# Seven block products instead of eight for gate and up of the first feed-forward stage, and a second product that sums four tiles in PSUM

## The chip, the cores and the metric

The kernel runs on one core of one Trainium2 chip. The metric is the device time of one execution in microseconds (us): 2367.63 us is the median of three runs of the kernel before, which lie between 2363.91 and 2369.41 us. All stages of the layer run in one launch. Engines are named as in the profile: PE is TensorE (matmuls), PEld its weight loads, DVE is VectorE, ACT is ScalarE, POOL is GpSimd, and SP is the engine whose queue issues all DMAs here.

## The reference

One inference step of one encoder layer. It computes, for 1024 prompt tokens and 64 sample tokens of width 1024,

```
h = x + 0.5 * rmsnorm(swiglu(rmsnorm(x), w_gate1, w_up1, w_down1))
m = token_mix(rmsnorm(h))          # latent attention and stick-breaking attention, 8 heads each
h = h + rmsnorm(m)
h = h + 0.5 * rmsnorm(swiglu(rmsnorm(h), w_gate2, w_up2, w_down2))
y = rmsnorm(h)
swiglu(x, wg, wu, wd) = (silu(x @ wg) * (x @ wu)) @ wd      # 1024 -> 2816 -> 1024, all float32
```

with a gain in every rmsnorm. Returned are y and the new rows of the attention's caches. The change touches the feed-forward blocks (swiglu) and nothing of the mathematics of the rest.

## The kernel before, in words

Features lie on the 128 partitions, tokens on the free axis. The 1088 tokens are two groups: G1 with 576 tokens (512 of the prompt and the sample), handled in two chunks of 288 columns, and G2 with 512 tokens in one chunk. A stream of four feed-forward stages runs through the kernel: block 1 of G1, block 1 of G2, block 2 of G1, block 2 of G2. A mixing stream (attention) is woven between the steps of the second and third of them (`weave`, L149: after each step of the first generator as many steps of the second as a debt counted in TensorE work allows). The first stage has no attention beside it.

Full precision is had from three passes: each operand is split into hi (a rounded copy, ACT) and lo (the rest, DVE, or POOL for some tiles), `split` on L115 to L125, and `mm3` (L158) issues three matmuls: hi by hi, hi by lo, lo by hi. A weight tile is loaded from HBM by SP, 128 x 512 at a time (`wr`, 4 buffers), and split into `wh` and `wl` of 128 x 1024, 4 buffers each (`weight`, L236).

`ffn` (L245) goes over the 22 tiles of 128 hidden features. For each it splits a gate tile and an up tile, and for each chunk of tokens sums eight k-tiles of mm3 into one PSUM bank for gate and one for up, then forms silu by Exp, Ln, Exp on ACT (L289 to L291), two multiplications on DVE that read PSUM (L292, L293) and a split into `hh` and `hl`. Two hidden tiles make a part. `down` (L252) is the second product: for each of 8 output tiles and each chunk it sums the two tiles of a part in PSUM (6 matmuls) and adds the bank to `y` on DVE (L265); it stands between the two hidden tiles of the next part. PSUM has 8 banks, four of them (`bank_f`) for the feed-forward stream and four for the mixing stream.

The start is in `body`: the two halves (288 tokens) of G1 are loaded and normalised (`rms_pe`, L200, and `scaled`, L221); after the first half the first step of the stage is issued (L911). `prep` (from L913) loads G2, takes its norm and forms x1, the hi and lo input of the second stage, between the steps of the first. `finish` (L838) of G1 and the mixing stream follow.

The order in which instructions stand in each engine's queue is set when the program is built: the emission order gives the priority, a planner with its own durations places an instruction where it finds it ready, and a tile's buffer is reused when all its readers are done. On the chip each queue runs in that fixed order.

Of the kernel before, what the change touches and what calls it, by code (L numbers as in the profile page):

```python
# [7 lines left out]
F32 = mybir.dt.float32  # L8
# [7 lines left out]
P = 128  # L16
D = 1024
KT = D // P
SEQ = 1024
# [15 lines left out]
# token groups: (first token, tokens, chunk of the moving axis). The tokens lie as  # L35
# the first half of the prompt, the sample, the second half of the prompt.
# [4 lines left out]
# TensorE work of the feed-forward stream for one unit of the mixing stream's, part by part  # L41
# [8 lines left out]
class Layer:  # L50
    def __init__(self, tc, ctx, a):
# [4 lines left out]
        self.turn = 0  # L56
        self.work = self.share = self.debt = 0.0
# [27 lines left out]
        # keys and values: group 1 (prompt | new), group 2, cached  # L85
# [28 lines left out]
    # x = hi + lo exactly; without x, lo holds the value and is replaced in place  # L114
# [12 lines left out]
    # TensorE work is counted, for the interleaving of the two streams  # L127
# [15 lines left out]
    # a step without TensorE work in the first stream makes room for some of the second's  # L143
# [4 lines left out]
    # the steps of the first stream, with the second one's between them: self.share of its work each  # L148
# [15 lines left out]
    # a bank of the feed-forward stream  # L164
# [3 lines left out]
    # a bank of the mixing stream  # L168
# [10 lines left out]
    # sum of squares, tile by tile  # L179
# [9 lines left out]
    # 1 / sqrt(mean over all features + eps), on every partition, from the sums of squares  # L189
# [9 lines left out]
    # the same with the sums over the tiles left to TensorE (T at most 512)  # L199
# [10 lines left out]
    # tmp() gives [P, T] tiles  # L210
# [9 lines left out]
    # hi and lo of gain * src * r  # L220
# [7 lines left out]
    # y := res + gain * y * r, for one tile of features  # L228
# [16 lines left out]
    def ffn(self, pool, tmp, n, g, xhi, xlo, y, end=None, tail=None):  # L245
# [4 lines left out]
        order = [(dt, c0, C) for dt in range(KT) for c0 in range(0, T, C)]  # L250

        def down(part, first, order, beside=iter(())):  # L252
            ws = [self.weight(pool, wd[mi]) for mi, _, _ in part]
            for dt, c0, C in order:
                ps = self.bank_f()
                for i, ((wh, wl), (_, hh, hl)) in enumerate(zip(ws, part)):
                    self.mm3(ps[:, :C], wh[:, dt * P:dt * P + P], wl[:, dt * P:dt * P + P],
                             hh[:, c0:c0 + C], hl[:, c0:c0 + C], i == 0, i == len(part) - 1)
                yield True
                next(beside, None)  # L260
                yy = y[:, dt, c0:c0 + C]
                if first:
                    nc.scalar.copy(yy, ps[:, :C])
                else:
                    nc.vector.tensor_tensor(yy, ps[:, :C], yy, op=ALU.add)  # L265

        for m in range(0, FT, 2):
            part = []
            for mi in (m, m + 1):
                if mi > m and pend:  # L270
                    yield from down(pend.pop(0), m == 2, order)
                gh, gl = self.weight(pool, wg[mi])
                uh, ul = self.weight(pool, wu[mi])
                hh = pool.tile([P, T], F32R, name="hh")
                hl = pool.tile([P, T], F32R, name="hl")
                for c0 in range(0, T, C):
                    cs = slice(c0, c0 + C)
                    pg = self.bank_f()
                    for k in range(KT):
                        ks = slice(k * P, k * P + P)  # L280
                        self.mm3(pg[:, :C], gh[:, ks], gl[:, ks], xhi[:, k, cs], xlo[:, k, cs], k == 0, k == KT - 1)
                        yield True
                    pu = self.bank_f()
                    for k in range(KT):
                        ks = slice(k * P, k * P + P)
                        self.mm3(pu[:, :C], uh[:, ks], ul[:, ks], xhi[:, k, cs], xlo[:, k, cs], k == 0, k == KT - 1)
                        yield True
                    s = tmp()[:, :C]
                    nc.scalar.activation(s, pg[:, :C], AF.Exp, scale=-1.0)  # L289
                    nc.scalar.activation(s, s, AF.Ln, bias=self.one)  # L290
                    nc.scalar.activation(s, s, AF.Exp, scale=-1.0)  # L291
                    nc.vector.tensor_tensor(s, pg[:, :C], s, op=ALU.mult)  # L292
                    nc.vector.tensor_tensor(s, pu[:, :C], s, op=ALU.mult)  # L293
                    self.split(hh[:, cs], hl[:, cs], x=s)
                part.append((mi, hh, hl))
# [4 lines left out]
        if tail:  # L300
            order = [(dt, c0, tail) for c0 in range(0, T, tail) for dt in range(KT)]
        yield from down(pend.pop(0), False, order, end)
# [18 lines left out]
        # query latent  # L321
# [13 lines left out]
        # rotary key: rows 64..95 the key, rows 96..127 its halves swapped  # L335
# [14 lines left out]
        # stick-breaking queries and keys, two heads per tile  # L350
# [31 lines left out]
        # key/value latent  # L382
# [14 lines left out]
        # stick-breaking values, tokens on the partitions  # L397
# [17 lines left out]
        # latent attention: keys and values  # L415
# [60 lines left out]
    def load_values(self, pool, pair, parts):  # L476
        """[128 keys, key tile, head, hi|lo, 64]"""
# [21 lines left out]
    def scores(self, ops, n):  # L499
        """ops: list of (lhsT, rhs tile); n keys in one or two equal halves."""  # L500
# [9 lines left out]
    def stick(self, pool, ps, nh, w, n, mask):  # L510
        """weights of stick-breaking attention from the scores; the last key is never visible."""
# [9 lines left out]
        # minus the log weight: v[j] = (z[j+1] + v[j+1]) - log_beta[j]  # L521
# [66 lines left out]
    def headnorm(self, pool, o, n, row, gi, c0, sums=None, turned=None):  # L588
        """per-head RMSNorm of two heads on the partitions; sums or turned: eps * (softmax sum)^2 of each query."""
# [88 lines left out]
    def sum_rows(self, pool, total, nb):  # L678
        """eps * sum^2 of each query, repeated over the 64 rows of its head."""
# [9 lines left out]
    def sample_pair(self, pool, kind, pair):  # L689
# [9 lines left out]
        for par in range(2):  # L699
# [6 lines left out]
            # queries of this head in its own half of the columns, zeros in the other  # L706
# [54 lines left out]
        if mla:  # L761
            # row r of lhsT holds query r % 64 of head r // 64: only its own head's rows count
# [8 lines left out]
    # output projection, post norm, the residual (left in y), and the statistics of the next norm  # L771
# [30 lines left out]
def body(tc, a, ctx):  # L802
# [35 lines left out]
    def finish(gi, y, n, bank):  # L838
        """post norm and residual of a feed-forward block; after the second the final norm"""
# [18 lines left out]
    def last(gi, y, res, pool, step):  # L858
        """the same in steps of tokens, with the residual at hand"""
# [22 lines left out]
    def work(pool, T, n=4):  # L882
        """tiles for passing use, weights, and accumulators of the mixing stream"""
# [5 lines left out]
    # first feed-forward block of group 1; the input norm of group 2 lies beside it  # L889
    T1, T2 = G1[1], G2[1]  # L890
    x1 = pair(fp, T2, "x")
    with tc.tile_pool(name="x0", bufs=1) as xp:
        x0 = pair(xp, T1, "x")
        y = ytile(T1)
        half = T1 // 2
        y0 = ytile(T1)
        zero = L.ffn(F, fact, 1, G1, *x0, y0)
        for c0 in (0, half):
# [8 lines left out]
            L.run(L.scaled(tmp, lambda k: y[:, k, cs], "pre1", r, x0[0][:, :, cs], x0[1][:, :, cs]))  # L907
            # what the first half of the tokens suffices for
# [4 lines left out]
        def prep():  # L913
# [4 lines left out]
            r = yield from L.rms(tmp, L.bank_f, (get(k) for k in range(KT)), T2, D)  # L918
            yield from L.scaled(tmp, get, "pre1", r, *x1)
# [3 lines left out]
        L.run(zero)  # L923
    rx = fp.tile([P, TM], F32, name="rx")[:, :T1]
# [88 lines left out]
def layout(inp):  # L1013
    """The arrays of the launch: the inputs in the order the chip reads them, and constants of the shapes."""
# [83 lines left out]
```

## Time and profile before

| | |
|---|---|
| runs: median (lowest to highest) | 2367.63 us (2363.91 to 2369.41) |
| the profiled execution, from its first to its last instruction (span) | 2367.6 us, the only time given for it |
| PE / PEld / DVE / ACT / POOL busy | 2283.5 / 2033.4 / 1539.0 / 1244.7 / 93.6 us |
| share of the chain that ended last | PE 69%, DVE 12%, ACT 9%, DMA 4%, issue 4% |

Busy is the time in which at least one instruction of the engine runs; matmuls overlap each other, so that a mean of 0.29 us for one does not say how often one starts. In a view by line, `out<-in` names the tiles written and read, `xN` is the number of instructions, then come the busy time in us and the mean ns of one, and behind the second bar the idle time ahead of them with what ended it. A view of stretches gives for each the busy time of every engine with its instructions, the TensorE clock granted (1.00 is full), the share of time that the DMA engines were busy, and GB/s.

### The profile page before, as it was taken

To read this page: it belongs to the slowest core of one execution; us is meant where nothing else is said; L and a number is where in the kernel's file an instruction comes from. 1 tells how busy PE (TensorE), PEld (TensorE's weight loads), DVE (VectorE), ACT (ScalarE), POOL (GpSimd) and SP (SyncE) were. 2 spreads that over 40 slices of the span, in tenths; PEclk is the share of its full clock that TensorE was granted. 3 is DMA by queue.
4 is the path that set the end of the run, shared out by engine and by line. 5 is a ranking of instruction groups with operands and counts; after the bars stand their busy time and mean duration, and the time that the engine had idled before them with its cause. 6 is when DMAs were issued, how large, how long until landed. Compare 5 with 4: busy or idle time off the path is not lost.

```text
span 2367.6 us, 37687 instructions
## 1 busy us (share of the span) xinstructions
PE 2283.5 (96%) x13869; PEld 2033.4 (86%) x13869; DVE 1539.0 (65%) x2743; ACT 1244.7 (53%) x2459; POOL 93.6 (4%) x270
## 2 busy tenths in 40 slices
PE   8999999989999999999999999999999999999997
PEld 7999999879987777788778999998888888888885
DVE  5555555764277878855873488888878588555555
ACT  6543333453367777754542477777776455433333
POOL 1000000010000000000110000000000010000001
PEclk9999999999999999999999999999999999999998
DMA  6322222445453343343444632323221424333321
GB/s 210 97 95 90 81 80 90 148 144 168 161 150 113 110 129 100 95 151 111 151 142 160 188 96 79 99 72 99 72 86 62 144 81 139 128 98 98 98 90 36
DMA packets 186615, 268.81 MB, mean 114 GB/s; under 512 B 59216, under 2 KB 68048, under 8 KB 186400
## 3 DMA queue, kind: packets, MB, share of 16 engines
q1 hardware_dynamic: 186432, 266.41, 35.8%
q8 instruction: 110, 1.80, 0.3%
q14 instruction: 73, 0.60, 0.1%
HBM read 227.61 MB, written 40.88 MB: 113 GB/s over the span
## 4 chain that ended last, share of the span: by engine, by line
PE 69%; DVE 12%; ACT 9%; DMA 4%; issue 4%; SPq 1%; POOL 1%; DVEq 0%; ACTq 0%; POOLq 0%
PE f L133 46%; PE s L133 11%; PE v L133 6%; PE t L133 3%; PE t L137 2%; DVE a L526 2%; DVE a L529 1%; ACT wh L121 1%; DVE a L520 1%; ACT a L517 1%; DVE wl L122 1%; ACT a L518 1%; ACT a L519 1%; DVE y L265 1%; DVE e L224 1%
## 5 line engine op out<-in xcount | busy, mean ns | idle before, releaser
L133 PE MATMUL f<-xh,wh 128*128 128x288 f32 (+1 forms) x2112 | 695.3, 329 | 4.4 <-ACT xh L121 2.8
L133 PE MATMUL f<-xl,wh 128*128 128x288 f32 (+1 forms) x2112 | 694.3, 329 | 2.9 <-POOL xl L122 1.8
L133 PE MATMUL f<-xh,wl 128*128 128x288 f32 (+1 forms) x2112 | 692.8, 328 | 0.0
L121 ACT CAST wh<-wr 128x512 fp32r<-128x512 f32 x638 | 374.2, 617 | 524.9 <-PE f L133 376.5
L122 DVE TENSOR_TENSOR wl<-wr,wh 128x512 fp32r<-128x512 f32 x638 | 431.2, 698 | 233.0 <-ACT wh L121 208.7
L133 PEld LDWEIGHTS f<-xl,wh 128*128 128x128 f32 x2112 | 397.7, 188 | 33.7 <-POOL xl L122 3.4
L133 PEld LDWEIGHTS f<-xh,wh 128*128 128x128 f32 x2112 | 397.6, 188 | 33.3 <-ACT xh L121 3.3
L133 PEld LDWEIGHTS f<-xh,wl 128*128 128x128 f32 x2112 | 397.5, 188 | 28.1 <-issue 0.8
L133 PE MATMUL f<-hh,wh 128*128 128x288 f32 (+2 forms) x1072 | 350.7, 328 | 6.6 <-ACT hh L121 3.2
L133 PE MATMUL f<-hl,wh 128*128 128x288 f32 (+2 forms) x1072 | 350.7, 327 | 0.0
L133 PE MATMUL f<-hh,wl 128*128 128x288 f32 (+2 forms) x1072 | 349.9, 327 | 0.2 <-DVE wl L122 0.2
L265 DVE TENSOR_TENSOR y<-f,y 128x288 f32<-128x288 f32 (+2 forms) x488 | 247.9, 523 | 85.4 <-PE f L133 83.8
L133 PEld LDWEIGHTS f<-hh,wh 128*128 128x128 f32 x1072 | 201.7, 189 | 23.4 <-ACT hh L121 4.0
L133 PEld LDWEIGHTS f<-hh,wl 128*128 128x128 f32 x1072 | 202.1, 189 | 14.3 <-issue 1.0
L133 PEld LDWEIGHTS f<-hl,wh 128*128 128x128 f32 x1072 | 202.1, 189 | 13.8 <-issue 0.8
L293 DVE TENSOR_TENSOR act<-f,act 128x288 f32<-128x288 f32 (+1 forms) x132 | 70.0, 531 | 92.6 <-PE f L133 91.8
L564 DVE TENSOR_TENSOR pl<-t,ph 128x384 fp32r<-128x384 f32 (+1 forms) x160 | 101.2, 633 | 35.6 <-ACT ph L563 31.2
L563 ACT CAST ph<-t 128x384 fp32r<-128x384 f32 (+1 forms) x160 | 86.7, 542 | 57.2 <-PE t L137 54.7
L292 DVE TENSOR_TENSOR act<-f,act 128x288 f32<-128x288 f32 (+1 forms) x132 | 69.8, 529 | 66.5 <-ACT act L291 66.4
L137 PE MATMUL t<-c_ident,a 128*128 128x128 f32 x616 | 106.0, 277 | 2.7 <-ACT a L531 0.9
L133 PE MATMUL s<-kh,qh 128*128 128x256 f32 (+3 forms) x224 | 84.4, 378 | 24.0 <-DVE a L529 16.1
L121 ACT CAST hh<-act 128x288 fp32r<-128x288 f32 (+1 forms) x132 | 64.8, 491 | 66.0 <-DVE act L293 65.9
(312 smaller groups left out, 3464.7 us busy)
## 6 DMA issues: line engine op xcount, KB each, us to landing
wr<-in_wg SPq DMA_DIRECT2D x176, 256.0 KB, 2.9
wr<-in_wu SPq DMA_DIRECT2D x176, 256.0 KB, 3.0
wr<-in_wd SPq DMA_DIRECT2D x176, 256.0 KB, 3.2
wr<-in_win SPq DMA_DIRECT2D x44, 256.0 KB, 3.3
kl<-ks SPq DMA_DIRECT2D x64, 128.0 KB, 2.8
wr<-in_wout SPq DMA_DIRECT2D x32, 256.0 KB, 2.8
h<-y SPq DMA_DIRECT2D x16, 288.0 KB, 2.3
p<-in_xT SPq DMA_DIRECT2D x16, 256.0 KB, 3.4
```

The costliest lines, as they stand in the source:

```text
L121: nc.scalar.copy(hi, x)
L122: eng.tensor_tensor(lo, x, f(hi), op=ALU.subtract)
L133: self.nc.tensor.matmul(out, lhsT=lhsT, rhs=rhs, start=start, stop=stop)
L137: self.nc.tensor.transpose(out, x, ident)
L224: self.nc.vector.scalar_tensor_tensor(x, src(k), self.gain(name, k), r, op0=ALU.mult, op1=ALU.mult)
L265: nc.vector.tensor_tensor(yy, ps[:, :C], yy, op=ALU.add)
L292: nc.vector.tensor_tensor(s, pg[:, :C], s, op=ALU.mult)
L293: nc.vector.tensor_tensor(s, pu[:, :C], s, op=ALU.mult)
L517: nc.scalar.activation(av, z, AF.Abs)
L526: nc.vector.tensor_tensor_scan(a[:, j0:n - 1][:, ::-1], zz[:, ::-1], a[:, j0:n - 1][:, ::-1], BIG, op0=ALU.add, op1=ALU.subtract)
L563: nc.scalar.copy(ph[:, end:], tr[:, end:])
L564: nc.vector.tensor_tensor(pl[:, end:], tr[:, end:], f(ph[:, end:]), op=ALU.subtract)
```

## The change

- In the first stage (block 1 of G1 alone) the gate product and the up product are formed for pairs of hidden tiles as a 2 x 2 block product: weights of two hidden tiles by two halves of the 1024 inputs, tokens in two halves of 288. Seven block products of four k-tiles stand for eight (`quad`). The weight combinations s1 to s4 are formed on POOL from raw tiles, each of the seven weight blocks (128 x 512) is then split; the seven products are put together by one copy on ACT and seven additions on DVE from PSUM into tiles in SBUF, on which silu works.
- The seven token blocks are formed at the start (`quarters`): two of them after the first half of the tokens, five after the second.
- These products rotate over all eight PSUM banks (`bank_q`).
- In all four stages weights are split in units of 128 x 512 (8 buffers of `wl` and `wh` in place of 4 of twice the size), hidden tiles are gathered in groups of four (22 = 5 x 4 + 2), and the second product sums four tiles (12 matmuls) in one PSUM bank before it is added to `y`. It takes its weights in two halves. `hh` and `hl` have 5 buffers in place of 3.
- x1 is no longer formed in the middle of the first stage but beside the last second product of that stage (`prepx`), since the new token blocks occupy its buffers until then.
- The scratch for dynamic DMA descriptors is set to 1024 bytes; comments are dropped.

```diff
+GROUP = 4
+    def unit(self, pool, src):
+        lo = pool.tile([P, 512], F32R, name="wl")
+        hi = pool.tile([P, 512], F32R, name="wh")
+        raw = pool.tile([P, 512], F32, name="wr")
+        self.nc.sync.dma_start(raw, src)
+        self.split(hi, lo, x=raw)
+        return hi, lo
+    def quad(self, pool, q, src, m, x, C, bank, use, first):
...
+        def combined(u, v, op):
+            t = q.tile([P, 512], F32, name="qs")
+            nc.gpsimd.tensor_tensor(t, u, v, op=op)
+            return t
+        def product(w, i):
...
+            self.split(hi, lo, x=w)
+            xh, xl = x[i]
+            ps = bank()[:, :C]
+            for k in range(H):
+                ks = slice(k * P, k * P + P)
+                self.mm3(ps, hi[:, ks], lo[:, ks], xh[:, k], xl[:, k], k == 0, k == H - 1)
+                yield True
+            return ps
...
+        a11, a21, a22 = raw(0, 0), raw(1, 0), raw(1, 1)
+        ps = yield from product(a11, 0)
+        c11 = part()
+        nc.scalar.copy(c11, ps)
+        a12 = raw(0, 1)
+        if first:
+            p2 = yield from product(a12, 1)
+        s1 = combined(a21, a22, ALU.add)
+        s2 = combined(s1, a11, ALU.subtract)
+        s3 = combined(a11, a21, ALU.subtract)
+        ps = yield from product(s2, 4)
+        u2 = part()
+        add(u2, ps, c11)
+        ps = yield from product(s3, 5)
+        u3 = part()
+        add(u3, ps, u2)
+        ps = yield from product(s1, 3)
+        c22 = part()
+        add(c22, ps, u3)
+        use(1, 1, c22)
+        add(u2, ps, u2)
+        s4 = combined(a12, s2, ALU.subtract)
+        if not first:
+            p2 = yield from product(a12, 1)
+        add(c11, p2, c11)
+        use(0, 0, c11)
+        ps = yield from product(a22, 6)
+        add(u3, ps, u3)
+        use(1, 0, u3)
+        ps = yield from product(s4, 2)
+        add(u2, ps, u2)
+        use(0, 1, u2)
+    def quarters(self, tmp, tiles, x, C, early):
...
+        if early:
+            for k in range(H):
+                b11, _, b21, _ = blocks(k)
+                put(0, k, b11)
+                put(1, k, b21, nc.gpsimd)
+            return
+        for k in range(H):
...
+            nc.vector.tensor_tensor(t1, b12, b11, op=ALU.subtract)
+            nc.vector.tensor_tensor(t2, b22, t1, op=ALU.subtract)
+            put(4, k, t2)
+            put(3, k, t1, nc.gpsimd)
+        for k in range(H):
...
+            nc.vector.tensor_tensor(t3, b22, b12, op=ALU.subtract)
+            put(5, k, t3)
+            nc.gpsimd.tensor_tensor(t4, b21, b11, op=ALU.subtract)
+            nc.vector.tensor_tensor(t4, t4, t3, op=ALU.subtract)
+            put(6, k, t4)
+            put(2, k, b22, nc.gpsimd if k % 2 else None)
     def ffn(...)
+        def product(part, ws, first, dt, c0, C):
+            ps = self.bank_f()
+            ks = slice(dt % H * P, dt % H * P + P)
+            for i, ((wh, wl), (_, hh, hl)) in enumerate(zip(ws, part)):
+                self.mm3(ps[:, :C], wh[:, ks], wl[:, ks], hh[:, c0:c0 + C], hl[:, c0:c0 + C],
+                         i == 0, i == len(part) - 1)
+            yield True
...
+        def down(part, first):
+            for half in range(2):
+                ws = [self.unit(pool, wd[mi][:, half * 512:half * 512 + 512]) for mi, _, _ in part]
+                for dt in range(half * H, half * H + H):
+                    for c0 in range(0, T, C):
+                        yield from product(part, ws, first, dt, c0, C)
...
+            first = self.quad(pool, q, wg, mi, xhi, half, self.bank_q, gate, early)
+            second = self.quad(pool, q, wu, mi, xhi, half, self.bank_q, up, early)
+            if early:
+                for steps in (first, second):
+                    for _ in range(2 * H):
+                        next(steps)
+                        yield True
+            yield from first
+            yield from between
+            yield from second
...
+        for m in range(0, FT, GROUP):
             part = []
+            if q:
+                for mi in range(m, min(m + GROUP, FT), 2):
+                    yield from double(mi, part, down(pend.pop(0), m == GROUP) if pend else ())
 def body(...)
-    sizes = {"wr": 4, "wl": 4, "wh": 4, "hh": 3, "hl": 3}
+    sizes = {"wr": 4, "wl": 8, "wh": 8, "hh": GROUP + 1, "hl": GROUP + 1}
+        def prepx():
+            x1.extend(pair(fp, T2, "x"))
+            tmp = lambda: xp.tile([P, T2], F32, name="p", bufs=4)
+            yield from L.scaled(tmp, streamed(tmp, xT[1]), "pre1", r1, *x1)
-            L.run(L.scaled(tmp, lambda k: y[:, k, cs], "pre1", r, x0[0][:, :, cs], x0[1][:, :, cs]))
+            for k in range(KT):
+                kk = k // 2 + k % 2 * H
+                nc.vector.scalar_tensor_tensor(y[:, kk, cs], y[:, kk, cs], L.gain("pre1", kk), r,
+                                               op0=ALU.mult, op1=ALU.mult)
+            L.quarters(tmp, [y[:, k] for k in range(KT)], x0, half, c0 == 0)
```

## Rows read from the trace of the kernel before

**Rows 1.** The page's first part: busy us, share of the span, instructions.

```profile
PE 2283.5 (96%) x13869; PEld 2033.4 (86%) x13869; DVE 1539.0 (65%) x2743; ACT 1244.7 (53%) x2459; POOL 93.6 (4%) x270
```

**Rows 2.** Stretches of the span: length, then PE, PEld, DVE, ACT, POOL, clock, DMA.

```profile
300.00:350.00 50.00, 50.00 (x380) 50.00 (x379) 26.96 (x54) 17.01 (x35) 0.00 (x0) 1.00 0.26 84
...
1150.00:1200.00 50.00, 43.85 (x279) 39.53 (x277) 46.93 (x73) 31.79 (x62) 8.72 (x6) 0.97 0.51 162
...
1500.00:1600.00 100.00, 96.23 (x686) 90.26 (x685) 85.88 (x155) 71.99 (x125) 2.87 (x20) 1.00 0.28 85
...
2100.00:2200.00 100.00, 100.00 (x443) 82.81 (x442) 50.83 (x79) 33.95 (x61) 0.00 (x0) 1.00 0.30 98
```

**Rows 3.** Chain of the first 470 us: start us, us, what (count).

```profile
33.61 0.81 POOL xl L122
...
34.46 398.99 PE f L133 x3002
```

**Rows 4.** What PE waited for, 1400 to 1900 us: total us, times, longest.

```profile
PE s L133 <- DVE a L529: 15.8, 25, 2.0
```

**Rows 5.** PE by line and form, 0 to 470 us: the first stage's matmuls.

```profile
L133 PE MATMUL f<-xh,wh 128*128 128x288 f32 x704 | 208.0, 296 | 2.8 <-ACT xh L121 2.8
...
L133 PE MATMUL f<-hh,wh 128*128 128x288 f32 x352 | 104.0, 296 | 0.2
```

**Rows 6.** DVE in order of time, 1164 to 1172 us: start us, us, instruction.

```profile
1164.38 1.83 DVE L122 TENSOR_TENSOR wl<-wr,wh 128x512 fp32r<-128x512 f32 x1
...
1170.36 0.45 DVE L292 TENSOR_TENSOR act<-f,act 128x288 f32<-128x288 f32 x1
1170.73 0.68 DVE L187 TENSOR_TENSOR tmp<-tmp 128x512 f32<-128x512 f32 x1
1171.33 0.45 DVE L293 TENSOR_TENSOR act<-f,act 128x288 f32<-128x288 f32 x1
```

**Rows 7.** POOL by form, whole span.

```profile
L122 POOL TENSOR_TENSOR xl<-p,xh 128x512 fp32r<-128x512 f32 x4 | 5.3, 1320 | 88.0 <-ACT xh L121 88.0
```

**Rows 8.** ACT by form, 100 to 400 us.

```profile
L121 ACT CAST wh<-wr 128x512 fp32r<-128x512 f32 x94 | 54.3, 616 | 119.1 <-PE f L133 119.1
L290 ACT ACTIVATE act<-act,ones 128x288 f32<-128x288 f32 x32 | 17.2, 536 | 0.5
L291 ACT ACTIVATE act<-act 128x288 f32<-128x288 f32 x32 | 14.2, 445 | 1.0
L121 ACT CAST hh<-act 128x288 fp32r<-128x288 f32 x31 | 13.3, 430 | 30.9 <-DVE act L293 30.9
L289 ACT ACTIVATE act<-f 128x288 f32<-128x288 f32 x31 | 12.6, 408 | 25.3 <-PE f L133 25.3
```

**Rows 9.** POOL in order of time at 1164 us.

```profile
1164.27 1.41 POOL L122 TENSOR_TENSOR xl<-tmp,xh 128x576 fp32r<-128x576 f32 x1 [3.01 <-ACT xh L121]
```

**Rows 10.** POOL, then DVE, in order of time at 113 us.

```profile
113.82 1.30 POOL L122 TENSOR_TENSOR xl<-p,xh 128x512 fp32r<-128x512 f32 x1 [4.59 <-ACT xh L121]
...
113.00 2.06 DVE L265 TENSOR_TENSOR y<-f,y 128x288 f32<-128x288 f32 x5
```

**Rows 11.** The start: DVE and POOL, then PE by form up to 34.46 us.

```profile
14.14 0.91 POOL L122 TENSOR_TENSOR xl<-t,xh 128x288 fp32r<-128x288 f32 x1 [13.70 <-ACT xh L121]
...
14.31 1.05 DVE L224 SCALAR_TENSOR_TENSOR t<-y,c_gains,r 128x288 f32<-128x288 f32 x1
...
26.78 1.37 DVE L224 SCALAR_TENSOR_TENSOR t<-y,c_gains,r 128x288 f32<-128x288 f32 x3
...
L133 PE MATMUL f<-xh,wh 128*128 128x288 f32 x25 | 7.7, 314 | 2.8 <-ACT xh L121 2.8
```

**Rows 12.** DVE by form, 100 to 400 us: x1 formed beside the first stage.

```profile
L224 DVE SCALAR_TENSOR_TENSOR p<-p,c_gains 128x512 f32<-128x512 f32 x8 | 6.0, 747 | 1.7 <-DMA p<-in_xT 1.7
```

**Rows 13.** DVE by form, whole span: the additions to y.

```profile
L265 DVE TENSOR_TENSOR y<-f,y 128x288 f32<-128x288 f32 x320 | 139.1, 451 | 42.9 <-PE f L133 42.0
L265 DVE TENSOR_TENSOR y<-f,y 128x512 f32<-128x512 f32 x152 | 102.3, 684 | 38.6 <-PE f L133 38.0
```

More of the change, by code (lines that the diff above doesn't have):

```diff
@@ L18 @@
 KT = D // P
+H = KT // 2
 SEQ = 1024
@@ L246, in ffn, with bank_q @@
+    def bank_q(self):
+        self.turn_q = (self.turn_q + 1) % 8
+        if self.turn_q < 4:
+            return self.bank_f()
+        if self.turn_q == 7:
+            return self.half_q
+        t = self.psa.tile([P, 2, 512] if self.turn_q == 6 else [P, 512], F32, name="vts"[self.turn_q - 4])
+        if self.turn_q < 6:
+            return t
+        self.half_q = t[:, 1]
+        return t[:, 0]
+    def ffn(self, pool, tmp, n, g, xhi, xlo, y, end=None, tail=None, q=None, stmp=None):
         nc, a = self.nc, self.a
@@ L249, in ffn @@
         pend = []
[L250 to L265, printed above, removed]
@@ L267, in ffn @@
-        for m in range(0, FT, 2):
-            part = []
[L269 to L295, printed above, removed]
@@ new lines, in units @@
+        def units(src):
+            return [self.unit(pool, src[:, i:i + 512]) for i in (0, 512)]
+        def product(part, ws, first, dt, c0, C):
[5 more added lines that the diff above has]
+            yield True
+            yy = y[:, dt, c0:c0 + C]
+            if first:
+                nc.scalar.copy(yy, ps[:, :C])
+            else:
+                nc.vector.tensor_tensor(yy, ps[:, :C], yy, op=ALU.add)
@@ new lines, in down, with down_last @@
+        def down(part, first):
[4 more added lines that the diff above has]
+                        yield from product(part, ws, first, dt, c0, C)
+        def down_last(part, step, beside):
+            ws = [[self.unit(pool, wd[mi][:, half * 512:half * 512 + 512]) for mi, _, _ in part] for half in range(2)]
+            if step:
+                order = [(dt, c0, step) for c0 in range(0, T, step) for dt in range(KT)]
+            else:
+                order = [(dt, c0, C) for dt in range(KT) for c0 in range(0, T, C)]
+            for dt, c0, n in order:
+                for _ in product(part, ws[dt // H], False, dt, c0, n):
+                    yield True
+                    next(beside, None)
@@ new lines, in silu, with double, gate, up @@
+        def silu(pg, s):
+            nc.scalar.activation(s, pg, AF.Exp, scale=-1.0)
+            nc.scalar.activation(s, s, AF.Ln, bias=self.one)
+            nc.scalar.activation(s, s, AF.Exp, scale=-1.0)
+            nc.vector.tensor_tensor(s, pg, s, op=ALU.mult)
+        def double(mi, part, between):
+            half = T // 2
+            sg = [stmp() for _ in range(2)]
+            hs = []
+            def gate(i, j, c):
+                silu(c, sg[i][:, j * half:j * half + half])
+            def up(i, j, c):
+                if not hs:
+                    hs.extend([pool.tile([P, T], F32R, name="hh"), pool.tile([P, T], F32R, name="hl")] for _ in range(2))
+                cs = slice(j * half, j * half + half)
+                nc.vector.tensor_tensor(sg[i][:, cs], c, sg[i][:, cs], op=ALU.mult)
+                self.split(hs[i][0][:, cs], hs[i][1][:, cs], x=sg[i][:, cs])
+            early = mi == 0
+            first = self.quad(pool, q, wg, mi, xhi, half, self.bank_q, gate, early)
[4 more added lines that the diff above has]
+                        next(steps)
+                        yield True
+            yield from first
+            yield from between
+            yield from second
+            part.extend((mi + i, *hs[i]) for i in range(2))
@@ L299, in ffn @@
         end = end() if end else iter(())
-        if tail:
-            order = [(dt, c0, tail) for c0 in range(0, T, tail) for dt in range(KT)]
-        yield from down(pend.pop(0), False, order, end)
+        yield from down_last(pend.pop(0), tail, end)
         self.run(end)
@@ L917, in prep @@
             get = streamed(tmp, xT[1])
-            r = yield from L.rms(tmp, L.bank_f, (get(k) for k in range(KT)), T2, D)
-            yield from L.scaled(tmp, get, "pre1", r, *x1)
+            yield from L.rms(tmp, L.bank_f, (get(k) for k in range(KT)), T2, D, r1)
         L.debt = 60.0
@@ L923, in body @@
         L.run(zero)
+    L.mixed = False
     rx = fp.tile([P, TM], F32, name="rx")[:, :T1]
```

68 lines of the change are left out of this document (62 added, 6 removed).

## The prediction, made before the changed kernel was run

> **What bounds the kernel now.** I read the page first, then the stretches, then the chain, and last single engines by form. The page shows PE busy for 96% of the span with VectorE at 65%, ScalarE at 53% and GpSimd at 4% [rows 1], which alone proves little, since busy matmuls overlap. So I went to stretches: in the first stage PE is busy 50.00 of 50 us at full clock while VectorE has 27 us of work, ScalarE 17 us, and the DMA engines 26% [rows 2]. The chain says the same: from 34.46 us on, for 398.99 us, nothing but 3002 matmuls; other engines end the waits only ahead of that, GpSimd last [rows 3]. In this stage a matmul that goes away is time that goes away, as long as the other engines keep up. In the stage with stick-breaking attention PE is busy 96% beside VectorE at 86%, and waits for VectorE there 15.8 us in all [rows 2, 4]. In block 2 of G2 it is 100% busy again [rows 2].
>
> All sums are made against the profiled execution's 2367.6 us, first to last instruction; that is the median of the runs (2367.63), so no correction is needed.
>
> **Part 1, the matmuls.** Before, a pair of hidden tiles takes 2 tiles x 2 matrices x 2 token halves x 8 k-tiles x 3 passes = 192 matmuls, 11 pairs make 2112, which is three times the 704 of one pass [rows 5]. Now it is 2 matrices x 7 products x 4 k-tiles x 3 = 168, that is 1848. 264 go. One starts every 50.00 / 380 = 0.1316 us [rows 2]: **-34.7 us**, if PE stays the bound. The second product keeps its 1056 matmuls (three times 352, [rows 5]).
>
> **Part 2, what VectorE, ScalarE and GpSimd get for it.** Take one quad (one matrix, one pair). PE: 84 x 0.1316 = 11.05 us. VectorE instructions in a full queue start 0.60 us apart at 128x512 and 0.37 us apart at 128x288, somewhat closer than their own durations [rows 6]. Seven splits and seven additions: 7 x 0.60 + 7 x 0.37 = 6.8 us; a gate quad has 4 multiplications more (8.3 us), an up quad 4 multiplications and 4 splits (9.8 us). GpSimd: 4 combinations at 1.32 us [rows 7], 5.3 us. ScalarE: 7 casts at 0.616, a copy (nearest is the read from PSUM at 0.408), in a gate quad four times 0.408 + 0.536 + 0.445, in an up quad four casts at 0.43 [rows 8]: 10.3 and 6.4 us. Taken singly each fits into 11.05 us.
>
> GpSimd and VectorE do not add up like that. At 1164.27 a GpSimd tensor_tensor of 1.41 us runs, and the split that VectorE starts at 1164.38 takes 1.83 us in place of 0.68: 1.15 us lost [rows 6, 9]. At 113.82 the same kind of GpSimd instruction runs beside additions that read PSUM, and five of them pass in 2.06 us, undisturbed [rows 10]. Of a quad's VectorE instructions only the seven additions read PSUM; the splits and, new, the multiplications (their operands now lie in SBUF) are of the disturbed kind. So each of the 16 combinations of a group (four quads) costs VectorE between 0 (it falls beside additions or idle time) and 1.15 us. The Trainium skill (SBUF — State Buffer, Who interferes with whom) calls this an exclusive lock between GpSimd and a VectorE instruction with two SBUF inputs, held for the whole instruction. The rows agree; by the rule alone a combination could cost VectorE its whole 1.32 us, not 1.15, and the first rival below would then come to 2416 us.
>
> How much PE feels of it: a group is four quads and one second product of 192 matmuls (25.3 us), which stands ahead of an up quad; then up, gate, up, gate follow without relief. In that run PE needs 44.2 us. VectorE needs 2 x 8.3 + 2 x 9.8 = 36.2 us and 16 times the loss s. At s = 0.5 it just keeps up, at 1.15 it is 10.4 us behind at the end. It starts with a lead: when the second product ends, four weight units lie ready in the eight buffers, 4 x 1.57 = 6.3 us of PE work, and PE can run on over eight banks before it needs an addition. In the second product VectorE has only 16 x 0.37 + 8 x 0.60 = 10.7 us to do in 25.3 us and gains the lead again. So PE loses 0 per group up to s = 0.9, and 4 us at 1.15: over 5.5 groups 0 to 22 us. I take **+8 us**, nearer the low end, since four instructions in ten are of the undisturbed kind, but not zero: the queues' orders are fixed without these losses, and where VectorE is at 86% PE already loses 4% [rows 2].
>
> **Part 3, the start.** Before, PE runs densely from 34.46 us, with some 71 stage matmuls (three times 23 to 25) done by then [rows 3, 11]. VectorE starts on the second half of the tokens at 26.78 [rows 11]. Now it has 8 scalings (in place), then 12 instructions for blocks 3 and 4, then 18 for blocks 5, 6 and 2: 8 x 0.46 (three in 1.37) + 30 x 0.37 = 14.8 us, and beside them GpSimd runs 10 instructions of 0.91 us and some of the combinations; the row at 14.31 shows a scaling of 1.05 us in place of 0.46, 0.6 us lost each [rows 11]. With about 10 us of that, all blocks are there at about 52 us. Until then PE can do the two early blocks for both matrices (48 matmuls), blocks 4 and 3 as they come (48) and a few more, about 115: 44 more than before, 5.8 us of work. So (52 - 34.5) - 5.8 = 11.7. I take **+11 us**, with bounds of +4 (half of the losses hidden) and +18 (none hidden, and products of the first pair cutting into the queue).
>
> **Part 4, the end of the stage.** Forming x1 cost PE nothing where it was, beside dense matmuls [rows 3, 12]. Now it lies beside 96 matmuls, 12.6 us, and may start only when the last quad has read its token blocks. VectorE: 8 scalings at 0.75, 4 splits at 0.60, 16 additions at 0.37 and up to four losses of 1.15 make 14.3 to 18.9 us; the next stage's first tile takes the k-tiles one by one over 24 x 0.226 = 5.4 us ([rows 2]: 443 in 100 us). 12.6 + 5.4 covers it nearly. The same kind of handover stands in the trace at 1150 to 1200 us and leaves PE idle 6.15 of 50 us [rows 2]. Bounds 0 to +9, taken **+4 us**.
>
> **Part 5, four tiles per bank in the other stages.** Matmuls stay the same. Additions to y at 128x288 go from 320 to 160, those at 128x512 from 152 to 72 [rows 13]. Of these 80 (30 us of VectorE at 0.37) and 40 (24 us at 0.60) lie in the two stages with attention beside them, where VectorE is partly waited for [rows 4]; the 40 of the last stage lie beside a PE that is 100% busy and save nothing. The steps woven into attention become twice as long (12 matmuls), which can hold up an attention matmul. Bounds -15 (all the wait for VectorE gone) and +8; taken **-4 us**. Smaller buffers of 128x512 carry the same bytes with the same number of loads, and DMA has room [rows 2]; the scratch size touches no transfer of this kernel, all of which SP issues: nothing.
>
> Sum: -34.7 + 8 + 11 + 4 - 4 = -15.7, so 2367.6 - 15.7 = **2352 us**. With all low bounds it would be 2322, with all high ones 2390.
>
> **Rivals.**
> *VectorE, held up by GpSimd, paces the quads (slower).* If the four ready units give no cover, because the fixed order puts splits behind additions that wait for PE, every run costs its full lag of 10.4 us: 57 in place of 8, 2401 us. It decides above s = 0.5 without cover, and above 0.9 with it. For it speaks the split of 1.83 us [rows 6, 9]; against it that casts of weights now wait for a free buffer, not for work (119.1 us of it) [rows 8], so splits do run ahead.
> *The conflict stays hidden and the start is short.* 0 to 2 us in part 2, +5 in part 3, -8 in part 5: 2335 us. For it speaks VectorE's rest of 23 us in 50 now [rows 2].
> *The gain is given back piecemeal:* 22 in part 2, 16 in part 3, +2 in part 5: about 2377; with milder values it ends on the old time.
> *The sum of four tiles does not help attention but holds it up:* if the wait of 15.8 us [rows 4] doubles, 2352 + 4 + 16 = 2372.
>
> **Chances.** A difference under 0.2% (4.7 us) cannot be told from none. Forecast 0.57 (its own range 2338 to 2362), full gain 0.17, given back 0.07 and attention held up 0.07 (both mostly within or just past the old time), VectorE as pacer 0.12. Faster 0.74, same 0.11, slower 0.15. The range goes from 2330, below the full gain, to 2384, which leaves out most of the pacer's case.
>
> **What would show it.** The first stage's gate and up matmuls at 1848, dense matmuls from about 50 us, the stage's last matmul near 430 us. In stretches of the first stage PE at 96 to 100% beside VectorE at 85 to 95% and GpSimd near 30%. Waits of PE for VectorE's wl or for a PSUM addition of the quads, if part 2 is larger. PE under 90% in those stretches, with VectorE never idle, would make the forecast wrong; so would a start that is dense before 40 us or after 60.

## The result and the profile after the change

The changed kernel takes 2402.47 us (median of four runs, 2396.97 to 2403.44) against 2368.52 us: slower by a ratio of 1.0137, 95% interval 1.0124 to 1.0150. The forecast was 2352 us in a range of 2330 to 2384: wrong in sign. The profiled execution spans 2400.4 us, 32.8 us more than that of before.

The page's first part for the changed kernel, to be read beside [rows 1]:

```profile
PE 2275.0 (95%) x13605; PEld 2017.3 (84%) x13605; DVE 1596.0 (66%) x2745; ACT 1310.5 (55%) x2563; POOL 229.6 (10%) x364
```

264 matmuls are gone (13869 to 13605), as worked out, and the span is longer all the same. Stretches of the changed kernel, columns as in [rows 2]:

```profile
0.00:100.00 100.00, 70.69 (x366) 60.93 (x367) 85.61 (x135) 54.61 (x122) 46.57 (x41) 0.81 0.43 138
100.00:420.00 320.00, 300.70 (x2211) 297.18 (x2210) 251.56 (x433) 156.38 (x329) 93.79 (x65) 0.99 0.29 89
...
300.00:350.00 50.00, 46.42 (x336) 45.95 (x335) 42.22 (x76) 27.76 (x59) 12.73 (x9) 0.97 0.32 101
```

and the same two long stretches of the kernel before:

```profile
0.00:100.00 100.00, 91.22 (x597) 84.88 (x598) 49.37 (x92) 57.49 (x129) 8.18 (x12) 0.97 0.49 156
100.00:420.00 320.00, 320.00 (x2410) 319.46 (x2409) 177.32 (x352) 115.19 (x239) 5.28 (x4) 1.00 0.28 89
```

Count the matmuls. By 100 us the changed kernel has issued 366, before it was 597: 231 behind, 30.4 us at 0.1316 us each. From 100 to 420 us it issues 2211 in place of 2410: 199 more, 26.2 us. The row of 300 to 350 us answers to the first of [rows 2]: PE idle 3.6 of 50 us where it was never idle, VectorE at 84%. The stage's end is to be read off its last second product, one row of the kernel before and one of the changed kernel (count, shortest, median and longest ns, first to last start in us):

```profile
L133 PE MATMUL f<-hl,wh x352: 290/295/298, 63.5 to 446.9; 128*128 128x288 f32 x176
```

```profile
L138 PE MATMUL f<-hl,wh x352: 290/295/606, 112.7 to 474.3; 128*128 128x288 f32 x176
```

446.9 became 474.3. So 27.4 of the 32.8 us arise in the first stage, though it has 34.7 us fewer matmuls: -34.7 + 30.4 (start) + 26.2 (middle) + 5.5 (the rest, the last quads). 5.4 us arise after it.

What PE waited for in the changed kernel, 0 to 480 us (total us, times, longest):

```profile
PE s L138 <- DVE qu L295: 20.1, 12, 4.0
PE f L138 <- ACT t L210: 7.7, 3, 4.3
PE s L138 <- ACT qu L300: 3.3, 2, 2.1
PE s L138 <- DVE wl L127: 3.2, 2, 1.7
```

The largest wait is for one PSUM tile alone, `s`, and for VectorE's additions (`qu`, line 295). `s` is the tile of two banks of the mixing stream, whose halves the new ring uses one right after the other. VectorE by form in the changed kernel, 100 to 420 us (busy, mean ns, then idle before):

```profile
L127 DVE TENSOR_TENSOR wl<-qs,wh 128x512 fp32r<-128x512 f32 x65 | 68.3, 1058 | 1.4 <-ACT wh L126 0.8
L127 DVE TENSOR_TENSOR wl<-qr,wh 128x512 fp32r<-128x512 f32 x49 | 41.4, 851 | 9.0 <-ACT wh L126 8.7
L295 DVE TENSOR_TENSOR qu<-f,qu 128x288 f32<-128x288 f32 x60 | 26.2, 446 | 0.9 <-PE f L138 0.9
L127 DVE TENSOR_TENSOR wl<-wr,wh 128x512 fp32r<-128x512 f32 x39 | 26.1, 682 | 2.7 <-ACT wh L126 2.7
L440 DVE TENSOR_TENSOR tmp<-qu,tmp 128x288 f32<-128x288 f32 x34 | 24.7, 725 | 0.0
L398 DVE TENSOR_TENSOR y<-f,y 128x288 f32<-128x288 f32 x48 | 21.6, 454 | 33.1 <-PE f L138 33.1
...
L425 DVE TENSOR_TENSOR tmp<-qu,tmp 128x288 f32<-128x288 f32 x34 | 15.4, 452 | 4.8 <-ACT tmp L424 4.7
```

Three forms with two inputs in SBUF are stretched most (1058 and 851 ns in place of 687, 725 in place of 454; the shorter figures are those of the run with the combinations on VectorE, below). What reads PSUM is not stretched (446, 454). Two inputs in SBUF alone stretch nothing: the splits of `wr` (682) and the gate's multiplications (L425, 452) have two as well, but in this trace only 3 of 39 and 2 of 34 of them run beside a GpSimd instruction, and they keep their length. Of the 65 splits of combinations, the 34 that run beside one take 1401 ns on average, the other 31 take 682. One wait in order of time in the changed kernel, VectorE, then GpSimd, then PE (start us, us):

```profile
158.45 0.44 DVE L295 TENSOR_TENSOR qu<-v,qu 128x288 f32<-128x288 f32 x1
158.81 1.69 DVE L127 TENSOR_TENSOR wl<-qs,wh 128x512 fp32r<-128x512 f32 x1
160.43 0.81 DVE L295 TENSOR_TENSOR qu<-t,qu 128x288 f32<-128x288 f32 x2
161.16 1.24 DVE L127 TENSOR_TENSOR wl<-qr,wh 128x512 fp32r<-128x512 f32 x1
162.32 0.45 DVE L295 TENSOR_TENSOR qu<-s,qu 128x288 f32<-128x288 f32 x1
...
158.66 1.30 POOL L276 TENSOR_TENSOR qs<-qs,qr 128x512 f32<-128x512 f32 x1 [0.68 <-POOL qs L276]
160.58 1.27 POOL L276 TENSOR_TENSOR qs<-qr 128x512 f32<-128x512 f32 x1 [0.62 <-DVE wl L127]
...
159.52 0.29 PE L138 MATMUL s<-qh,wl 128*128 128x288 f32 x1
...
160.19 0.29 PE L138 MATMUL f<-ql,wh 128*128 128x288 f32 x1
162.82 0.40 PE L138 MATMUL s<-xh,wh 128*128 128x288 f32 x1 [2.34 <-DVE qu L295]
```

The product in the first half of `s` ends behind 159.52. The next product, in the other half, starts at 162.82, right after the addition at 162.32 that reads the first half. Five matmuls of a third product stand between in PE's queue; they cover some 0.7 us. The addition comes late since two of the instructions ahead of it, splits that stood against GpSimd, took 1.69 and 1.24 us.

### The profile page after: what moved, and what is told of

Same layout as the page of the kernel before. It is cut to its first block, busy times and chain, and to the rows that moved or that the text cites. A ratio compares the mean times of both kernels' runs of the same rounds, so it can differ in the third digit from the quotient of the medians.

```text
span 2400.4 us, 37758 instructions
## 1 busy us (share of the span) xinstructions
PE 2275.0 (95%) x13605; PEld 2017.3 (84%) x13605; DVE 1596.0 (66%) x2745; ACT 1310.5 (55%) x2563; POOL 229.6 (10%) x364
## 4 chain that ended last, share of the span: by engine, by line
PE 53%; DVE 9%; issue 6%; ACT 6%; DMA 2%; POOL 1%; SPq 0%; DVEq 0%; ACTq 0%; POOLq 0%
PE f L138 32%; PE s L138 10%; PE v L138 6%; PE t L138 3%; PE t L142 3%; DVE a L713 2%; DVE a L716 1%; DVE a L707 1%; DMA e<-h 1%; ACT a L706 1%; ACT a L704 1%; ACT a L705 1%; DVE pl L751 1%; DVE wl L127 1%; ACT wh L126 0%
## 5 line engine op out<-in xcount | busy, mean ns | idle before, releaser
L138 PE MATMUL f<-xh,wh 128*128 128x288 f32 (+1 forms) x1576 | 538.5, 342 | 5.5 <-DVE y L398 2.9
L138 PE MATMUL f<-xl,wh 128*128 128x288 f32 (+1 forms) x1576 | 537.9, 341 | 1.3 <-POOL xl L127 0.9
L138 PE MATMUL f<-xh,wl 128*128 128x288 f32 (+1 forms) x1576 | 535.6, 340 | 1.4 <-DVE wl L127 1.4
L127 DVE TENSOR_TENSOR wl<-wr,wh 128x512 fp32r<-128x512 f32 x550 | 374.9, 694 | 202.0 <-ACT wh L126 156.9
L138 PEld LDWEIGHTS f<-xh,wh 128*128 128x128 f32 x1576 | 298.3, 189 | 34.7 <-ACT act L422 3.1
L138 PEld LDWEIGHTS f<-xl,wh 128*128 128x128 f32 x1576 | 298.6, 189 | 29.8 <-issue 1.2
L138 PEld LDWEIGHTS f<-xh,wl 128*128 128x128 f32 x1576 | 298.4, 189 | 29.2 <-DVE wl L127 1.8
L398 DVE TENSOR_TENSOR y<-f,y 128x288 f32<-128x288 f32 (+2 forms) x248 | 126.6, 517 | 101.9 <-PE f L138 101.0
L142 PEld LDWEIGHTS t<-c_ident,a 128*128 128x128 f32 x616 | 71.1, 140 | 29.9 <-issue 8.2
L138 PE MATMUL v<-pl,v 128*128 128x256 f32 x320 | 93.6, 314 | 0.6
```

Source lines behind the costliest of these rows:

```text
L127: eng.tensor_tensor(lo, x, f(hi), op=ALU.subtract)
L138: self.nc.tensor.matmul(out, lhsT=lhsT, rhs=rhs, start=start, stop=stop)
L142: self.nc.tensor.transpose(out, x, ident)
```

## The experiments

**The sum of four tiles alone.**

```diff
-        zero = L.ffn(F, fact, 1, G1, x0, None, y0, end=prepx, q=qpool(xp), stmp=ftmp(T1))
+        zero = L.ffn(F, fact, 1, G1, *x0, y0)
...
```

(and the loading of the tokens and `prep` as in the kernel before)

> The first stage is the eight-product one of before, with x1 formed in its middle; units of 128x512, groups of four and the sum of four tiles stay as in the changed kernel. Theory 'the first stage alone lost it': 2360 to 2368 us, since VectorE loses a few tens of us of additions and nothing else changes. Rival 'the sum of four tiles holds up the other stages': 2373 us or more, with the stretches from 500 to 700 us as poor as in the changed kernel.

2369.68 us, ratio to before 1.0013 (1.0004 to 1.0022). Between the two expectations; the sum of four tiles with the smaller units gains nothing. Its stretch of 1400 to 1900 us against that of the kernel before:

```profile
1400.00:1900.00 500.00, 480.87 (x3298) 445.60 (x3299) 368.22 (x630) 348.02 (x617) 12.84 (x87) 1.00 0.29 88
```

```profile
1400.00:1900.00 500.00, 479.47 (x3295) 444.31 (x3294) 389.15 (x686) 339.91 (x603) 12.88 (x87) 1.00 0.28 88
```

VectorE has 21 us less to do and PE does the same number of matmuls.

**GpSimd's combinations left out.**

```diff
         def combined(u, v, op):
-            t = q.tile([P, 512], F32, name="qs")
-            nc.gpsimd.tensor_tensor(t, u, v, op=op)
-            return t
+            return u
...
-                return pool.tile(shape, dt, name=name, bufs={"qr": 6, "qs": 4, "qu": 8}[name])
+                return pool.tile(shape, dt, name=name, bufs={"qr": 10, "qu": 8}[name])
```

> The changed kernel without GpSimd's 88 weight combinations: s1 to s4 are left out, the raw tile stands in their place, and the raw tiles have 10 buffers; products, splits and additions are all there. Theory 'port' (VectorE's splits and multiplications wait for GpSimd): the 24 us lost between 100 and 420 us go nearly all, and some 8 us at the start: 2365 to 2375 us, splits back at 0.69 us. Theory 'VectorE simply has too much to do in a quad' (banks freed late by its additions): splits get shorter but PE still waits for the quads' additions: 2388 us or more.

2362.20 us, ratio 0.9972 (0.9962 to 0.9983): 40 us less than the changed kernel, more than the port theory said. PE is busy 317.62 us of 100 to 420. With the ring and the start as they are, this is about the most that a change to the combinations alone can give.

**The combinations on VectorE.**

```diff
-            nc.gpsimd.tensor_tensor(t, u, v, op=op)
+            nc.vector.tensor_tensor(t, u, v, op=op)
```

> The changed kernel with the 88 weight combinations on VectorE. It adds 88 x 0.60 = 53 us of VectorE work and takes away 88 losses at the port. Theory 'port', with a loss of about 0.75 us for each combination (66 us in all): 2385 to 2400 us, a little faster than the changed kernel. Theory 'too much to do on VectorE': 53 us more work on the bound, 2420 us or more.

2368.32 us, ratio 0.9999 (0.9989 to 1.0008). Some 53 us more work for VectorE, and 34 us less time: VectorE's amount of work is not the bound. The gain is beyond both theories, which is where the port alone began to look too small a cause. Its stretch from 100 to 420 us, its splits there, and PE's first matmul form into `s` with the idle time ahead of it:

```profile
100.00:420.00 320.00, 319.06 (x2389) 317.65 (x2388) 258.74 (x525) 162.06 (x339) 0.00 (x0) 1.00 0.31 94
...
L127 DVE TENSOR_TENSOR wl<-qs,wh 128x512 fp32r<-128x512 f32 x68 | 45.8, 687 | 0.5 <-ACT wh L126 0.2
...
L138 PE MATMUL s<-xh,wh 128*128 128x288 f32 x68 | 20.6, 303 | 0.9 <-ACT qu L300 0.5 <-DVE qu L295 0.3
```

VectorE is busy longer (258.74 us) than in the changed kernel (251.56), its splits take 687 ns, and PE is full. The ring is the same, with the two halves of `s` one after the other, and yet PE waits for an addition of `s` 0.3 us in this stretch, where it waited 16.0 us in the changed kernel: when the additions come in time, the ring costs next to nothing.

**The start cut down.**

```diff
-            put(4, k, t2)
-            put(3, k, t1, nc.gpsimd)
...
+            put(2, k, b12)
+            put(3, k, b22, nc.gpsimd)
...
+        return b + [b[2], b[3], b[2]]
```

> The changed kernel with the start cut down: of the five token blocks of the second half only two are formed (plain splits of the two quarters of the second half), the others are left out and the products read these instead; the number of products is the same. Theory 'the start costs about 30 us' (VectorE behind GpSimd, and matmuls at half clock): 2378 to 2388 us. Theory 'the start only delays what VectorE has to do anyway': 2395 us or more.

2386.69 us, ratio 1.0081 (1.0066 to 1.0096), 16 us less than the changed kernel, although PE's waits for `s` by an addition grew to 24.4 us. By 100 us it has issued 439 matmuls, 73 more than the changed kernel (9.6 us).

**No GpSimd in the start either.**

```diff
-                put(1, k, b21, nc.gpsimd)
+                put(1, k, b21)
-            nc.gpsimd.tensor_tensor(t4, b21, b11, op=ALU.subtract)
+            nc.vector.tensor_tensor(t4, b21, b11, op=ALU.subtract)
```

(and `put(3, ...)` and `put(2, ...)` likewise, on top of the combinations on VectorE)

> As the run with the combinations on VectorE (2368.3 us), and GpSimd's part of the start (14 splits and 4 differences of 128x288) on VectorE too. Theory 'port': 18 x 0.37 = 6.7 us of VectorE work are added and 18 losses of about 0.6 us go: 2360 to 2366 us, all blocks ready some 4 us sooner. Rival 'in the start GpSimd helps, VectorE is the bound': 2372 us or more.

2365.39 us, ratio 0.9989 (0.9980 to 0.9999), within what the port theory said: 3 us less than with the combinations alone on VectorE. The intervals of these two runs overlap, so this gain is not shown beyond the noise.

**Six single banks, combinations back on GpSimd.**

```diff
-        self.turn_q = (self.turn_q + 1) % 8
+        self.turn_q = (self.turn_q + 1) % 6
         if self.turn_q < 4:
             return self.bank_f()
-        if self.turn_q == 7:
-            return self.half_q
...
+        return self.psa.tile([P, 512], F32, name="vt"[self.turn_q - 4])
```

> The changed kernel with its combinations on GpSimd, the quads' products rotating over six PSUM tiles of one bank each in place of eight of which two share a tile. Theory 'port': the place where PE waits moves, the loss stays: 2398 to 2410 us. Rival 'the tile of two banks, which comes free only when both its products have been added, makes the waits' (PE waited 16 us for it between 100 and 475 us): 2385 us or less.

2373.72 us, ratio 1.0027 (1.0016 to 1.0038): the rival's time is right, and the theory that the port alone makes the loss falls. The losses at the port are all still there:

```profile
100.00:420.00 320.00, 315.68 (x2350) 312.83 (x2349) 261.46 (x457) 159.27 (x340) 92.78 (x65) 1.00 0.30 92
...
L127 DVE TENSOR_TENSOR wl<-qs,wh 128x512 fp32r<-128x512 f32 x68 | 76.8, 1136 | 1.5 <-ACT wh L126 1.3
```

Splits at 1136 ns, even longer than in the changed kernel, and yet PE is busy 315.68 of 320 us, with fewer banks. It issues 2350 matmuls there, 139 more than the changed kernel.

**The halves of the shared tile four products apart.** Eight banks, only the order of the ring is another.

```diff
+        what = "sffvhfft"[self.turn_q]      # s, h: the two halves
...
```

> The changed kernel with its combinations on GpSimd and all eight banks; only the order of the ring differs: the two halves of the two-bank tile are four products apart instead of next to each other. Theory 'a product into the second half waits for the addition that reads the first half, which comes late when GpSimd holds VectorE up': the waits of PE for that tile go, 2368 to 2380 us, splits still stretched to over 1 us. Rival 'eight banks with a shared tile come free too late altogether, six single ones were better for another reason': 2392 us or more.

2377.51 us, ratio 1.0040 (1.0024 to 1.0055), 25 us less than the changed kernel from the order of the ring alone. PE's wait for `s` by an addition, 20.1 us in the changed kernel, is here

```profile
PE s L138 <- DVE qu L295: 8.0, 7, 2.7
```

while PE is nearly full and splits take 1103 ns:

```profile
100.00:420.00 320.00, 316.12 (x2358) 314.18 (x2357) 261.16 (x457) 158.95 (x339) 93.88 (x65) 1.00 0.30 93
...
L127 DVE TENSOR_TENSOR wl<-qs,wh 128x512 fp32r<-128x512 f32 x68 | 74.6, 1103 | 1.6 <-ACT wh L126 1.3
```

So it is not the number of banks, and not the port alone. The loss takes both: additions that come late, and a product that waits for the addition behind the product just before it.

**Groups of two with the combinations on VectorE.**

```diff
-GROUP = 4
+GROUP = 2
...
```

> The combinations on VectorE, and groups of two hidden tiles in all stages, so that a second product of 96 matmuls stands in every pair: Strassen without the sum of four tiles. Theory 'groups of four have no part in the gain' (the sum of four alone gave 1.0013): 2364 to 2371 us. Rival 'four quads in a row without relief, and the missing additions, matter once VectorE has the combinations': 2376 us or more.

2374.29 us, ratio 1.0026 (1.0015 to 1.0038), between the two expectations again, 6 us slower than with groups of four. Its first stage is not the slower one (it ends at 439.8 us against 442.6), so the run doesn't test what it was meant to; why the later stages lose stays open.

**The first pair by eight products.** Nothing on GpSimd as above; while PE does the first pair of hidden tiles as the kernel before does, VectorE forms the blocks.

```diff
+                if m == 0:
+                    yield from classic(0, part)
+                    form()
+                    yield from classic(1, part)
-                for mi in range(m, min(m + GROUP, FT), 2):
+                for mi in range(m + 2 * (m == 0), min(m + GROUP, FT), 2):
...
```

> No GpSimd in the first stage's combinations and blocks, and the first pair of hidden tiles computed by the eight products of before, while VectorE forms the seven token blocks beside it: 24 matmuls more than the changed kernel (+3.2 us), but the start should be as dense as before. Theory 'the start costs some 20 us of waiting that other work can cover': 2346 to 2354 us, faster than both kernels. Rival 'VectorE pays for it later' (32 instructions of 0.37 us more beside the first pair): 2360 us or more.

2354.57 us, ratio 0.9946 (0.9933 to 0.9959): **faster than both kernels**. It does 24 matmuls more than the run without GpSimd (3.2 us) and takes 10.8 us less. Its first two stretches and the end of its stage:

```profile
0.00:100.00 100.00, 85.61 (x552) 80.46 (x553) 81.45 (x180) 65.41 (x150) 0.20 (x4) 0.95 0.53 168
100.00:420.00 320.00, 318.12 (x2371) 315.38 (x2370) 259.35 (x526) 159.15 (x330) 2.69 (x2) 1.00 0.29 89
...
L138 PE MATMUL f<-hl,wh x352: 290/295/403, 90.1 to 425.6; 128*128 128x288 f32 x176
```

552 matmuls by 100 us where before had 597 and the changed kernel 366; the stage ends at 425.6, 21.3 us sooner than before. Not all of that is kept: this execution, the slowest of its five runs, spans 2357.4 us, 10.2 less than before, so what follows the stage takes 1931.8 us where it took 1920.7. In the changed kernel and the nine runs with groups of four it takes 1920.7 to 1931.8 us, although these runs differ from the changed kernel in the start and the first stage only. Each edit makes the planner set a new order of the queues; whether that is the reason wasn't tested. A few us between two runs are therefore no proof of what an edit in the first stage does.

**The same with six single banks.** The ring of e6 in that version.

```diff
-        self.turn_q = (self.turn_q + 1) % 8
+        self.turn_q = (self.turn_q + 1) % 6
...
```

> The version with no GpSimd in blocks and combinations and the first pair by eight products (2354.6 us), with six single banks. Theory: without the losses at the port the shared tile costs nothing, 2350 to 2358 us. Rival 'both halves of the remedy add': 2345 us or less.

2356.51 us, ratio 0.9948 (0.9936 to 0.9961): no different. The cases together, medians in us, first with the halves next to each other, then with single banks: 2402.5 and 2373.7 with GpSimd's combinations; 2354.6 and 2356.5 without GpSimd and with the first pair by eight products. This second pair has another start too. With the start of the changed kernel there is one case with the combinations on VectorE, 2368.3, with the halves next to each other; its counterpart with single banks wasn't run. In these cases the ring matters only when additions come late, and late additions matter much only with that ring.

## Why the prediction was wrong, step by step

Measured against the forecast's sum of -15.7, the span's +32.8 is 48.5 us too much: 18.2 of it in part 2 (26.2 in place of 8), 19.4 in part 3 (30.4 in place of 11), and 10.9 at the end of the stage and behind it, where parts 4 and 5 together stood at nothing.

**Part 1, the matmuls: right.** 264 are gone. Where PE is nearly full in the middle of the stage (316 to 319 us of 320 in the runs above), the stage keeps the gain; once the start is covered as well, it ends 21.3 us sooner than before (the first pair by eight products).

**Part 2, VectorE and GpSimd: the first failing step.** The loss at the port was sized well. From 100 to 420 us the four stretched forms lose 65 x 0.37 + 49 x 0.16 + 34 x 0.27 (rows above) and 35 x 0.09 (the splits of the hidden tiles), 44 us over GpSimd's 65 instructions: 0.68 us for each, inside the 0 to 1.15 given and below the 0.9 up to which PE was to lose nothing. PE lost 26 us of matmuls there nevertheless. What failed is the sentence that "PE can run on over eight banks before it needs an addition". Two of the eight are halves of one tile, and the product in the second half waits for the addition that reads the first; there PE runs on over no bank at all, only over the few matmuls that the fixed order puts in between. I had read the ring in the change and counted its banks, not what each product waits for. The Trainium skill's lock (SBUF — State Buffer, Who interferes with whom) agrees with these runs (splits of 687 ns without GpSimd, of up to 1136 ns on average with it; PSUM readers unchanged), but by itself it prices the wrong thing. With single banks the same losses stand, PE is idle 4.3 of 320 us and issues 2350 matmuls in place of 2410: 60 fewer, 7.9 us, near the 8 that were forecast.

**The first rival** gave 2401 us and the time is 2402.5. That is luck. Its mechanism was VectorE as the bound of the quads, and it isn't: VectorE was given 53 us more work and the kernel became faster, and with single banks every loss stayed in place and 29 us came back. At the measured loss of 0.68 us its own sum would not give 2401 either: a run would lag 36.2 + 16 x 0.68 - 44.2 = 2.9 us, 16 us over 5.5 groups, which makes 2360.

**Part 3, the start: the second failing step, far too small.** 30.4 us in place of 11. The blocks were ready when forecast:

```profile
51.12 0.44 DVE L127 TENSOR_TENSOR xl<-t,xh 128x288 fp32r<-128x288 f32 x1
```

is the last of them, against "about 52". The two stretches that meet there, of the kernel before and then of the changed one:

```profile
0.00:52.00 52.00, 43.22 (x235) 36.88 (x236) 29.53 (x56) 31.78 (x72) 8.18 (x12) 0.93 0.63 203
52.00:100.00 48.00, 48.00 (x364) 48.00 (x363) 19.83 (x37) 25.71 (x58) 0.00 (x0) 1.00 0.33 105
```

```profile
0.00:52.00 52.00, 31.00 (x110) 22.59 (x110) 38.11 (x63) 27.83 (x64) 21.80 (x24) 0.74 0.56 178
52.00:100.00 48.00, 39.69 (x256) 38.35 (x257) 47.50 (x73) 26.78 (x58) 24.77 (x17) 0.89 0.30 95
```

At 52 us the changed kernel is 125 matmuls behind, 16.5 us where the sum had 11.7: 78 of the stage's matmuls had been issued by then, not "about 115". Behind 52 us, where the sum put nothing, it falls back by another 108, 14.2 us. Two things were missed. Until the blocks were ready PE's matmuls arrived in drops, and its clock fell to half; and being ready was not the end of it, since VectorE went on behind its queue. In the changed kernel:

```profile
35.00:55.00 20.00, 11.03 (x35) 8.43 (x36) 20.00 (x32) 8.58 (x20) 10.54 (x10) 0.50 0.22 53
55.00:85.00 30.00, 26.77 (x192) 25.67 (x191) 29.50 (x47) 18.19 (x42) 15.99 (x11) 0.99 0.30 96
85.00:95.00 10.00, 5.50 (x24) 5.26 (x25) 10.00 (x15) 4.96 (x12) 5.74 (x4) 0.74 0.34 107
```

VectorE is busy 59.5 of these 60 us, and PE issues 251 matmuls, where 60 / 0.1316 = 456 would go. At 90.4 us the wait for `s` strikes as well, 4.0 us, the longest of it. Two runs take a part of it away, the cut-down start and the single banks:

```profile
0.00:100.00 100.00, 77.32 (x439) 69.63 (x440) 83.81 (x130) 56.66 (x124) 42.35 (x36) 0.88 0.50 159
```

```profile
0.00:100.00 100.00, 76.56 (x413) 66.18 (x414) 84.53 (x135) 54.58 (x123) 47.44 (x41) 0.83 0.43 137
```

Against 366 matmuls that is 9.6 us for forming fewer blocks and 6.2 us for the shared tile; how much of the rest is the clock wasn't separated.

**Part 4, the end: the term for x1 was not needed.** PE's waits in the changed kernel from 460 to 520 us, around the end of the stage at 474.3:

```profile
PE s L138 <- ACT e L638: 3.5, 1, 3.5
PE f L138 <- DVE hl L127: 0.3, 1, 0.3
PE t L138 <- DVE tmp L192: 0.2, 1, 0.2
```

None of them is for x1's tiles (`xh`, `xl`), for which 4 us was forecast, and the longest stands in the kernel before too (3.4 us). Between 420 us and the end of the stage the changed kernel loses 5.5 us, after the stage 5.4 us. The run with the sum of four tiles alone is 3 us slower than before (1.0013), so a part of the 5.4 may come with that; what the rest is stays open.

**Part 5, the sum of four tiles: wrong in sign, by little.** Forecast -4, measured 1.0013, that is +3 us (+1 to +5). VectorE's load fell (389 to 368 us in 1400 to 1900); PE's waits there stayed: in the changed kernel 15.2 us for the scan's line against 15.8 in [rows 4]. The additions that went were not what PE waited for. Why the time rose is not shown.

## What to carry to other kernels

When a change rotates more products over PSUM, list for each bank what its next product waits for: in this program halves of one tile, used one after the other, make a product wait for the addition of the one before, however many banks there are. An engine's lost time (here some 44 us at the port) costs the bound engine little while there is slack between producer and consumer (7.9 us with single banks), and more than half of it when a tight dependency takes the slack away (26 us); so look for the dependency before sizing the loss. Small work that shares the port with VectorE can be better off on VectorE itself, though that engine is the busier one: 34 us here. A start-up that needs all its inputs transformed before the new scheme runs can be covered by doing the first piece of work the old way: 10.8 us here.

## What the runs showed of the hardware that was not expected

With this ring VectorE at 81%, with the combinations as work of its own (258.74 of 320 us), leaves PE full (319.06), while VectorE at 79% with GpSimd beside it (251.56 of 320 us) does not (300.70). And the clock: in 35 to 55 us of the changed kernel PE, busy 11 of 20 us in short drops, was granted 0.50, that is 1.2 of 2.4 GHz; within a drop matmuls start 0.24 us apart there and not 0.13, so here a thin supply also slowed what did get through.
